# Order of products and of state updates in the scan phase of a two-mixer linear-attention block

## The chip, the cores and the metric

One core of one Trainium2 chip runs the whole layer as one program. The metric is the device time of one execution in microseconds (us); a kernel's time is the median of its runs.

## What is computed

The layer reads 2048 latent tokens and a prefix of 256 context tokens, 1024 channels each. After a modulated norm and one wide projection, two linear-attention mixers run over both, each in both directions: GLA (a decay for each key channel) and Gated DeltaNet (GDN, a decay for each head and the delta rule). The part of the reference that the change touches, cut to its core:

```
def gla_chunked(q, k, v, g, s0):                 # 4 heads, key width 64, value width 128
    bc = cumsum(g within a chunk)
    def step(s, (qi, ki, vi, bi)):
        dec = exp(where(causal, bi[t] - bi[s], -inf))          # for each key channel
        att = einsum('bhtd,bhsd,bhtsd->bhts', qi, ki, dec)
        o = (qi * exp(bi)) @ s + att @ vi
        s_new = s * exp(bl) + (ki * exp(bl - bi)).T @ vi
def gdn_chunked(q, k, v, g, beta, s0):           # 4 heads, widths 128
    ...                                          # u, w, aqk solved ahead of the scan
    def step(s, (qi, ki, ui, wi, ai, gi)):
        v_new = ui - wi @ s
        o = (qi * exp(gi)) @ s + ai @ v_new
        s_new = s * exp(gl) + (ki * exp(gl - gi)).T @ v_new
oa = gla(forward) + rev(gla(backward));  ob = gdn(forward) + rev(gdn(backward))
out = (gate_a * (norm(oa) * silu(ag)) @ w_gla + gate_b * (norm(ob) * silu(bg)) @ w_gdn) @ w_o
return rmsnorm(x + gt * out)
```
Each latent scan starts from the last context state of its own direction. The states after the last latent chunk are not returned.

## The kernel before

The program first projects all tokens (L365, every fp32 product as three products of rounded halves), then convolves, normalises and solves the triangular systems of GDN. The scan phase, `phase_mix`, comes next, and at its end the merge of the mixers (L1519) and the output projection (L1588). All work is written for one core; a scheduler (Tile) sets the order on each engine from the order in which the code issues, and inserts the waits.

Chunks have 128 tokens here: 2 of context and 16 of latents. `phase_mix` makes 17 steps. In step s it prepares GLA's chunk pair (2 + s forward, 17 - s backward), while the scans of the pair that step s - 1 prepared run beside it; the 17th step, the closing one, only scans, beside the first work of the merge. Each piece of work is a Python generator, and `weave` takes them in turn by their weights (12 for `gdn_scan`, 8 for `gla_scan`, 20 for `gla_step`). From the ninth step on both directions of a chunk have been seen, so a finished chunk also runs through `finish` (squares on ScalarE, a product on GpSimd at L1347, transposes at L1352). These steps are the second half below.

GLA's scores inside a chunk (`at`, both directions at once) come level by level: at level m (64, 32, 16, 8, 4, 2, 1) a token pair that a block border of size m separates gets `sum over channels of q * exp(to the border) * k * exp(from the border)`. `gla_group` makes the factors of two levels: sums of gates on TensorE (L1110, fp32r), exponentials on ScalarE (L1192, L1195), the product with q on VectorE (L1201, into `ql`) and with k on GpSimd (L1202, into `E`). `gla_ones` makes level 1, where a factor is the exponential of one token's gate: four transposes (L1213), exponentials (L1215), one VectorE product of 128x256 (L1216). Then `gla_lev` multiplies one level: 64 key channels of one head stand on one half of the rows, so each of its four products uses 64 of the 128 rows of the array (L1226), into one of two slots of the PSUM tile `lv`; a predicated copy on VectorE (L1233), or two copies on ScalarE for level 64 (L1230), takes the pairs of that level into `at`.

`gla_scan` does one chunk in one direction: the update of the 64x128 states in four products that each use half of the columns (L1282), the state read by VectorE, then the output: `at` with v on the whole array (L1306, forward chunk only) and the state product on half of the rows (L1310), added to `prev`, the output of the other direction read back from memory, into `oi`. `gdn_scan` does the same for GDN with whole-array products (L1042, L1053, L1063, L1072 for the state, L1082). `gla_ends`, `gla_kt` and `gla_qe` make the factors at the chunk's ends (L1110, L1128, L1134).

A product of fp32 numbers leaves two records in the trace, a transpose or an fp32r product one. In the profile's rows `64*128` means 64 rows by 128 columns of the array in use; `pz`, `pe` and `pm` are PSUM buffers and `Sa`, `Sb` the states.

Of the kernel before, what the change touches and what calls it, by code (L numbers as in the profile page):

```python
# [11 lines left out]
F32 = mybir.dt.float32  # L12
# [5 lines left out]
ALU = mybir.AluOpType  # L18
# [4 lines left out]
P = 128  # L23
# [7 lines left out]
NCTX = CTX // P  # L31
# [65 lines left out]
class Build:  # L97
# [933 lines left out]
    def gdn_scan(self, r, need_o):  # L1031
# [16 lines left out]
        if need_o:  # L1048
# [5 lines left out]
            oi = self.op.tile(B4, F32, name="oi", bufs=4)  # L1054
# [12 lines left out]
        S2 = self.st.tile(B4, F32, name=f"Sb{d}")  # L1067
        if S is not None:
            nc.gpsimd.tensor_tensor(S2, S, self.bc(self.egl, c, d), op=ALU.mult)
        ps = self.heads(self.pv())  # L1070
        for h in range(4):
            nc.tensor.matmul(ps[:, h], r["kt"][:, h], vn[:, h], start=True, stop=True)  # L1072
        if S is None:
            nc.vector.tensor_copy(S2, ps)
        else:
            nc.vector.tensor_tensor(S2, S2, ps, op=ALU.add)
        self.Sb[d] = S2
        yield
# [90 lines left out]

    def gla_ctx(self, pairs):  # L1170
# [35 lines left out]
    def gla_ones(self, r):  # L1206
        nc, k = self.nc, r["k"]
        E = self.gE.tile([P, 2, P], F32, name="E1", bufs=1)
        ql = self.gq.tile([P, 2, P], F32, name="ql1", bufs=1)
# [6 lines left out]
        nc.vector.tensor_tensor(ql, E, r["q"], op=ALU.mult)  # L1216
        return [(r["at"], [k[:, ct] for ct in range(2)], ql, 1)]

    def gla_lev(self, at, ks, ql, m):
        nc = self.nc  # L1220
        ps = self.slot()
        at = self.byhalf(at)
        for ct in range(2):
            for hp in range(2):
                rows = slice(64 * hp, 64 * hp + 64)
                nc.tensor.matmul(ps[:, hp, ct], ks[ct][rows], ql[rows, ct], start=True, stop=True)  # L1226
        if m == 64:
            for x in range(2):
                rows, cols = slice(64 * x, 64 * x + 64), slice(64 - 64 * x, 128 - 64 * x)
                nc.scalar.copy(at[rows, :, :, cols], ps[rows, :, :, cols])  # L1230
        else:
            i = LEVELS.index(m) - 1
            nc.vector.copy_predicated(at, self.am[:, i].unsqueeze(1).unsqueeze(1).broadcast_to([P, 2, 2, P]), ps)  # L1233

    def gla_step(self, f, b):
# [9 lines left out]
        todo = yield from self.gla_group(f, 0)  # L1245
        self.gla_ends(b)
        yield
        todo += yield from self.gla_group(f, 2)
# [3 lines left out]
        self.gla_lev(*todo.pop(0))  # L1252
        yield
        more = self.gla_group(f, 4)
        next(more)
        yield
        self.gla_lev(*todo.pop(0))
        yield
        try:
            next(more)  # L1260
            next(more)
        except StopIteration as e:
            todo += e.value
        yield
        self.gla_kt(b)
        self.gla_lev(*todo.pop(0))
        yield
        todo += self.gla_ones(f)
        self.gla_qe(f)
        while todo:  # L1270
            yield
            self.gla_lev(*todo.pop(0))
        yield

    def gla_scan(self, r, need_o):
        nc, wk = self.nc, self.wk
        d, c = r["d"], r["c"]
        S = self.Sa[d]
        ps = self.pv()
        for h in range(4):  # L1280
            ct, hp = h // 2, h % 2
            nc.tensor.matmul(ps[64 * hp:64 * hp + 64, ct * P:(ct + 1) * P], r["kt"][:, 64 * h:64 * h + 64],  # L1282
                             r["v"][:, h * P:(h + 1) * P], start=True, stop=True)
        S2 = self.st.tile([P, 2, P], F32, name=f"Sa{d}")
        for ct in range(2):
# [349 lines left out]
```

## Time and profile before

| what | value |
|---|---|
| median of 3 runs | 2199.81 us (2198.74 to 2201.21) |
| profiled execution | 2198.7 us, span 2196.9 us, mean granted clock 0.989 |
| scan phase in the trace | about 1375 to 1805 us |
| L1110 in it, both halves of the gates | 74.3 + 67.2 us busy |
| L1226, both kinds of factors | 68.7 + 11.4 us busy, 15.2 idle ahead |
| L1282, L1306, L1310 | 27.0, 18.1, 15.6 + 14.1 us busy |
| bytes moved | 315.68 MB, mean 144 GB/s |

The engines are named PE (TensorE; PEld is its loading of weights), DVE (VectorE), ACT (ScalarE), POOL (GpSimd) and SP (SyncE, which issues the DMAs). Busy time of PE counts each record from its start to its modelled end, and records overlap: a record of 128 columns counts with about 0.27 us. So the pace is read from the starts. A row `A <- B at L: us, times, us each` of the waits says that A's engine stood idle, and that B's instruction at line L ended that wait.

### The profile page before, as it was taken

What the parts mean: (1) busy time and instruction counts of PE and PEld (TensorE: products, weight loads), DVE (VectorE), ACT (ScalarE), POOL (GpSimd) and SP (SyncE); (2) the same over time, 40 slices, a digit from 0 to 9 for tenths busy, and PEclk for the clock granted to TensorE, in tenths of its full rate; (3) what the DMA queues carried; (4) which work ended last, traced back from release to release, by engine and by line L of the source; (5) the groups of instructions that cost most, each with busy time, mean ns of one, the idle gap of its engine ahead of it and who ended that gap; (6) DMA issues with size and microseconds to landing.
All of it is one profiled execution on the core that took longest, in us unless ns stands there. A gap on an engine that the chain in (4) does not pass through costs nothing. (4 is left out here: it accounts for less than half of the span.)

```text
span 2196.9 us, 40078 instructions
## 1 busy us (share of the span) xinstructions
PE 2122.3 (97%) x15168; PEld 1764.3 (80%) x15168; DVE 1245.2 (57%) x2178; ACT 884.2 (40%) x2188; POOL 858.2 (39%) x765
## 2 busy tenths in 40 slices
PE   5999999999999999999999998999999988999998
PEld 2688888888888888777777776888878877999888
DVE  3813555567776554655555554666777776444333
ACT  3654255455542223443434443444544444111211
POOL 2410122222320115665666662555555554322331
PEclk8999999999999999999999999999999999999999
DMA  8323122222222234443444435888688858433322
GB/s 281 104 89 115 53 60 68 63 63 61 70 75 74 83 89 137 140 141 116 134 150 145 146 134 174 281 303 277 227 267 287 263 176 254 138 120 125 101 80 84
DMA packets 275005, 315.68 MB, mean 144 GB/s; under 512 B 22280, under 2 KB 206716, under 8 KB 274812
## 3 DMA queue, kind: packets, MB, share of 16 engines
q1 hardware_dynamic: 274812, 313.12, 44.4%
q8 instruction: 120, 1.97, 0.4%
q14 instruction: 73, 0.60, 0.1%
HBM read 203.20 MB, written 109.84 MB: 142 GB/s over the span
## 5 line engine op out<-in xcount | busy, mean ns | idle before, releaser
L365 PE MATMUL pz<-hi,wh 128*128 128x512 f32 (+1 forms) x1560 | 621.3, 399 | 1.7 <-DVE hi L133 1.7
L365 PE MATMUL pz<-lo,wh 128*128 128x512 f32 (+1 forms) x1560 | 600.3, 385 | 1.8 <-POOL lo L134 1.8
L365 PE MATMUL pz<-hi,wl 128*128 128x512 f32 (+1 forms) x1520 | 588.0, 387 | 0.0
L365 PEld LDWEIGHTS pz<-lo,wh 128*128 128x128 f32 x1560 | 294.5, 189 | 51.0 <-POOL lo L134 3.6
L365 PEld LDWEIGHTS pz<-hi,wh 128*128 128x128 f32 x1560 | 294.2, 189 | 48.0 <-DVE hi L133 2.5
L365 PEld LDWEIGHTS pz<-hi,wl 128*128 128x128 f32 x1520 | 286.2, 188 | 53.7 <-issue 0.4
L134 POOL TENSOR_TENSOR wl<-w,wh 128x1024 fp32r<-128x1024 f32 x44 | 110.6, 2514 | 436.2 <-ACT wh L131 311.9
L563 DVE SCALAR_TENSOR_TENSOR acc<-zpad,cw,acc 128x1024 f32<-128x1024 f32 x192 | 268.2, 1397 | 6.7
L1519 PE MATMUL pm<-yh,wab 128*128 128x256 f32 x1024 | 187.9, 284 | 4.4 <-DVE mt L1523 4.4
L867 DVE CAST_PREDICATED U<-kit,pl 128x256 f16<-128x256 int32 x216 | 91.3, 432 | 138.7 <-PE pl L990 134.9
L1519 PEld LDWEIGHTS pm<-yh,wab 128*128 128x128 f32 x1024 | 161.3, 193 | 5.1 <-ACT wo L131 4.7
L1588 PE MATMUL pz<-wo,mh 128*128 128x512 f32 (+1 forms) x528 | 161.2, 388 | 0.0
L1519 PE MATMUL pm<-yl,wab 128*128 128x256 f32 x512 | 145.7, 285 | 0.8 <-POOL yl L134 0.8
L983 ACT CAST ppb<-pl 128x256 f16<-128x256 f32 x216 | 73.6, 374 | 166.4 <-PE pl L982 160.0
L1588 PEld LDWEIGHTS pz<-wo,mh 128*128 128x128 f32 x528 | 98.4, 189 | 20.2
L134 DVE TENSOR_TENSOR sql<-sq,sqh 128x512 fp32r<-128x512 f32 (+1 forms) x36 | 28.0, 805 | 141.6 <-ACT sqh L131 141.4
L618 POOL TENSOR_TENSOR acc<-acc,sq 128x512 f32<-128x512 f32 x32 | 50.2, 1576 | 138.4 <-ACT sq L617 78.6
L1588 PE MATMUL pz<-wo,ml 128*128 128x512 f32 (+1 forms) x264 | 101.8, 386 | 0.0
L1519 PEld LDWEIGHTS pm<-yl,wab 128*128 128x128 f32 x512 | 98.7, 193 | 1.7 <-POOL yl L134 1.2
L1202 POOL TENSOR_TENSOR E<-E,ak 128x256 f32<-128x256 f32 x96 | 76.8, 820 | 58.9 <-ACT E L1192 44.7
L134 POOL TENSOR_TENSOR yl<-wr,yh 128x1024 fp32r<-128x1024 f32 x16 | 40.3, 2542 | 134.2 <-ACT yh L131 134.2
L1233 DVE COPY_PREDICATED at<-am,lv 128x512 f32<-128x512 int32 x96 | 70.5, 734 | 31.5 <-PE lv L1226 29.4
(292 smaller groups left out, 4190.5 us busy)
## 6 DMA issues: line engine op xcount, KB each, us to landing
dgate<-ob SPq DMA_DIRECT2D x96, 256.0 KB
gd<-dgd SPq DMA_DIRECT2D x32, 768.0 KB
w<-in_w_in SPq DMA_DIRECT2D x44, 512.0 KB
qk<-dqkv SPq DMA_DIRECT2D x32, 512.0 KB
ga<-dgate SPq DMA_DIRECT2D x64, 256.0 KB
dqkv<-acc SPq DMA_DIRECT2D x192, 64.0 KB
dgd<-tm SPq DMA_DIRECT2D x36, 256.0 KB
dgd<-n SPq DMA_DIRECT2D x36, 256.0 KB
```

The lines of the kernel that those rows point to most:

```text
L134: getattr(nc, lo).tensor_tensor(dst_lo, src, dst_hi.bitcast(F32), op=ALU.subtract)
L365: nc.tensor.matmul(ps[:, 0:n], a[:, kk, :], b[:, kk, :], start=(k == 0), stop=(k == last - 1))
L563: nc.vector.scalar_tensor_tensor(acc, src, wcol, acc, op0=ALU.mult, op1=ALU.add)
L618: nc.gpsimd.tensor_tensor(v, v, r, op=ALU.mult)
L867: self.nc.vector.copy_predicated(out, mv, data)
L983: nc.scalar.copy(ppl, pc.rearrange("p h (j i) -> p h j i", i=m))
L1202: nc.gpsimd.tensor_tensor(E[:, :, li, 1], E[:, :, li, 1], k, op=ALU.mult)
L1233: nc.vector.copy_predicated(at, self.am[:, i].unsqueeze(1).unsqueeze(1).broadcast_to([P, 2, 2, P]), ps)
L1519: nc.tensor.matmul(ps[:, half * 256:half * 256 + 256], wab[wi][:, k, j * P:(j + 1) * P], yy[:, k, :], start=(i == 0), stop=(i == 11))
L1588: nc.tensor.matmul(ps, aa[:, k, i * P:(i + 1) * P], wo[k][wi][:, cs], start=(j == 0), stop=(j == 23))
```

## The change

1. `gla_lev` takes two levels at once: eight half-row products one after the other, then their evictions.
2. `gla_scan` is split. `gla_state` updates both directions' states in one run of eight half-column products (L1303), and is called from inside `gla_step` of the next pair. `gla_out` makes the outputs of both chunks in one run: four whole products (L1321) and eight half-row ones (L1326, directly ahead of the first two levels), into two PSUM tiles, and two VectorE additions into one tile `og`. `prev` of both chunks is one tile too. `gla_step`'s weight goes from 20 to 24.
3. Level 1 is no longer a product of matrices. For neighbours t and t - 1 the score of a head is the sum over its 64 channels of `q * k * exp(gate)`. `gla_ones` makes that elementwise product (two VectorE halves at L1224, and GpSimd with k at L1225), and `gla_near` sums it over the two halves of the rows by a product with a 128x2 matrix of ones and zeros, `bones` (L1232), of which a predicated copy (L1234) takes the right entries.
4. In the closing step GDN's last states are not updated (`end=True`: no L1070, L1073), nor GLA's (`gla_end` calls `gla_out` alone).

The names below carry the numbers that the two programs give to their tiles. TensorE in a first-half step, before: the second half of the levels, from the first product of the next scan (L1042) on.

```order
L1042 MATMUL pz<-Sb_16664,qk 128x128
L1226 MATMUL lv<-ql,E 128x128 x4
L1042 MATMUL pz<-Sb_16664,qk 128x128 x3
L1042 MATMUL pz<-Sb_16672,qk 128x128
L1226 MATMUL lv<-ql,E 128x128 x4
L1042 MATMUL pz<-Sb_16672,qk 128x128 x3
L1110 MATMUL pe<-wt,gh_16819 128x256
L1110 MATMUL pe<-wt,gl_16820 128x256
L1110 MATMUL pe<-wt,gh_16819 128x256
L1226 MATMUL lv<-ql,E 128x128 x4
L1110 MATMUL pe<-wt,gl_16820 128x256
L1282 MATMUL pz<-av,akt 64x128 x7
```
After, the same place:

```order
L1042 MATMUL pz<-Sb_16945,qk 128x128
L1220 MATMUL pe<-kf,g_16785 128x128
L1244 MATMUL lv<-ql,E 128x128 x8
L1220 MATMUL pe<-kf,g_16785 128x128 x3
L1042 MATMUL pz<-Sb_16945,qk 128x128 x3
L1042 MATMUL pz<-Sb_16953,qk 128x128 x4
L1244 MATMUL lv<-ql,E 128x128 x8
L1232 MATMUL pe<-bones,qk_17064 128x2 x2
L1111 MATMUL pe<-wt,gh_17118 128x256
```
The half-row products stand in groups of eight instead of four, and the next step's first gate sums (L1111) now stand behind L1232. Earlier in the same step, after:

```order
L1083 MATMUL pz<-vn,gd 128x128 x8
L1321 MATMUL pz<-av,at 128x128 x4
L1326 MATMUL pz<-Sa_16557,q_16484 128x128 x4
L1326 MATMUL pz<-Sa_16560,q_16490 128x128 x4
L1244 MATMUL lv<-ql,E 128x128 x8
L1111 MATMUL pe<-wt,gh_16813 128x2x128
```
Outputs and the first two levels form one run of 16 half-row products. GpSimd in a second-half step, before (L1202 is the factor with k, L1347 the finishing product, L1134 `gla_qe`):

```order
L1347 TENSOR_TENSOR oi<-oi,fss 128x512
L1202 TENSOR_TENSOR E<-E,ak_19271 128x2x128 x2
L1347 TENSOR_TENSOR oi<-oi,fss 128x512
L1134 TENSOR_TENSOR q_19273<-E_19327,q_19273 128x256
L1347 TENSOR_TENSOR oi<-oi,fss 128x512
L134 TENSOR_TENSOR gl_20085<-g_20056,gh_20084 128x512
```
After:

```order
L1209 TENSOR_TENSOR E<-E,ak_18478 128x2x128 x2
L1384 TENSOR_TENSOR og<-og,fss 128x512
L1225 TENSOR_TENSOR qk_18751<-qk_18751,ak_18478 128x256
L1135 TENSOR_TENSOR q_18480<-E_18534,q_18480 128x256
L1384 TENSOR_TENSOR oi<-oi,fss 128x512 x2
L134 TENSOR_TENSOR gl_19273<-g_19244,gh_19272 128x512
L1384 TENSOR_TENSOR og<-og,fss 128x512
```
The new product L1225 stands behind the first finishing product and ahead of `gla_qe`. ScalarE in that step, after:

```order
L1381 ACTIVATE fy,fss<-og 128x128 x3
L1381 ACTIVATE fy,fss<-oi 128x128
L1382 ACTIVATE fss<-fss,cb 128x4
L1381 ACTIVATE fy,fss<-oi 128x128
L1383 ACTIVATE fss<-fss 128x4
L1222 ACTIVATE E_18750<-pe 128x128 x2
```
Level 1's exponentials (L1222) stand behind the squares of the finishing work.

The diff, cut to its core:

```diff
-    def gdn_scan(self, r, need_o):
+    def gdn_scan(self, r, need_o, end=False):
...
-            oi = self.op.tile(B4, F32, name="oi", bufs=4)
+            oi = self.op.tile(B4, F32, name="oi")
...
+        if not end:
             S2 = self.st.tile(B4, F32, name=f"Sb{d}")
...
     def gla_ones(self, r):
...
-        nc.vector.tensor_tensor(ql, E, r["q"], op=ALU.mult)
-        return [(r["at"], [k[:, ct] for ct in range(2)], ql, 1)]
+        for d in range(2):
+            nc.vector.tensor_tensor(w[:, :, d:P:2], E[:, :, 1 - d:P:2], q[:, :, 1 - d:P:2], op=ALU.mult)
+        nc.gpsimd.tensor_tensor(w, w, k, op=ALU.mult)
+        return w
+
+    def gla_near(self, at, w):
+        nc = self.nc
+        pd = self.pe()
+        for ct in range(2):
+            nc.tensor.matmul(pd[:, 2 * ct:2 * ct + 2], w[:, ct], self.bones, start=True, stop=True)
+        B = [P, 4, P]
+        nc.vector.copy_predicated(at, self.am[:, len(LEVELS) - 2].unsqueeze(1).broadcast_to(B),
+                                  pd[:, 0:4].unsqueeze(2).broadcast_to(B))
+
+    def gla_lev(self, levs):
+        nc, got = self.nc, []
+        for at, ks, ql, m in levs:
+            ps = self.slot()
...
+            got.append((self.byhalf(at), ps, m))
+        for at, ps, m in got:
...
-    def gla_step(self, f, b):
+    def gla_step(self, f, b, prev):
...
+        if prev is not None:
+            S = self.gla_state(prev)
+            yield
+        levs = yield from self.gla_group(f, 0)
         self.gla_ends(b)
         yield
+        more = yield from self.gla_group(f, 2)
         self.gla_kt(f)
         self.gla_qe(b)
         yield
+        if prev is not None:
+            done = self.gla_out(prev, S)
+        self.gla_lev(levs)
+        if prev is not None:
+            done()
+            yield
+            yield from self.gla_put(prev)
+        yield
+        last = yield from self.gla_group(f, 4)
+        yield
+        self.gla_lev(more)
         yield
         self.gla_kt(b)
+        w = self.gla_ones(f)
         self.gla_qe(f)
+        yield
+        self.gla_lev(last)
+        yield
+        self.gla_near(f["at"], w)
+        yield
...
+    def gla_out(self, pair, S):
+        nc = self.nc
+        f = pair[0]
+        po = [self.pv().rearrange("p (d c t) -> p d c t", d=2, c=2) for _ in range(2)]
         for h in range(4):
+            nc.tensor.matmul(po[h % 2][:, 0, h // 2], f["at"][:, h], f["v"][:, h * P:(h + 1) * P],
+                             start=h < 2, stop=False, skip_group_check=True)
+        for d, r in enumerate(pair):
             for h in range(4):
                 ct, rows = h // 2, slice(64 * (h % 2), 64 * (h % 2) + 64)
+                nc.tensor.matmul(po[h % 2][:, d, ct], r["qe"][rows, ct], S[d][rows, ct], start=False,
+                                 stop=d == 1 and h >= 2, skip_group_check=True)
...
-                for (a, b) in prev:
-                    gens.append((self.gdn_scan(b, True), 12))
-                    gens.append((self.gla_scan(a, True), 8))
+                for x in prev:
+                    gens.append((self.gdn_scan(x[1], True, si == len(order)), 12))
+                if si == len(order):
+                    gens.append((self.gla_end(pair), 4))
...
-                gens.append((self.gla_step(*[x[0] for x in cur]), 20))
+                gens.append((self.gla_step(*[x[0] for x in cur], pair if si else None), 24))
```

More of the change, by code (lines that the diff above doesn't have):

```diff
@@ L1066, in gdn_scan @@
         yield
[L1067 to L1078, printed above, removed]
+        if not end:
+            S2 = self.st.tile(B4, F32, name=f"Sb{d}")
+            if S is not None:
+                nc.gpsimd.tensor_tensor(S2, S, self.bc(self.egl, c, d), op=ALU.mult)
+            ps = self.heads(self.pv())
+            for h in range(4):
+                nc.tensor.matmul(ps[:, h], r["kt"][:, h], vn[:, h], start=True, stop=True)
+            if S is None:
+                nc.vector.tensor_copy(S2, ps)
+            else:
+                nc.vector.tensor_tensor(S2, S2, ps, op=ALU.add)
+            self.Sb[d] = S2
+            yield
         if need_o:
@@ L1168, in ctx_loads, with gla_ctx_states @@
         return [[(self.gla0[d, d ^ i], gdn[d, d ^ i]) for d in range(2)] for i in range(2)], rest
+    def gla_ctx_states(self, pairs):
+        for p in pairs:
+            self.gla_state([x[0] for x in p])
+            yield
+            yield
     def gla_ctx(self, pairs):
@@ new lines, in gla_step, with gla_state @@
+        self.gla_lev(last)
+        yield
+        self.gla_near(f["at"], w)
+        yield
+    def gla_state(self, pair):
+        nc = self.nc
+        S = list(self.Sa)
+        ps = self.pv()
+        for d, r in enumerate(pair):
+            for h in range(4):
+                ct, hp = h // 2, h % 2
+                nc.tensor.matmul(ps[64 * hp:64 * hp + 64, (2 * d + ct) * P:(2 * d + ct + 1) * P],
+                                 r["kt"][:, 64 * h:64 * h + 64], r["v"][:, h * P:(h + 1) * P], start=True, stop=True)
+        for d, r in enumerate(pair):
+            S2 = self.Sa[d] = self.st.tile([P, 2, P], F32, name=f"Sa{d}")
+            for ct in range(2):
+                pc = ps[:, (2 * d + ct) * P:(2 * d + ct + 1) * P]
+                if S[d] is None:
+                    nc.vector.tensor_copy(S2[:, ct], pc)
+                else:
+                    nc.vector.scalar_tensor_tensor(S2[:, ct], S[d][:, ct], r["dec"][:, ct:ct + 1], pc,
+                                                   op0=ALU.mult, op1=ALU.add)
+        return S
@@ new lines, in gla_out, with gla_put, gla_end, gla_prev @@
+        return done
+    def gla_put(self, pair):
+        for d, r in enumerate(pair):
+            yield from self.put_o(0, r["c"] - NCTX, self.og[:, d])
+    def gla_end(self, pair):
+        self.gla_out(pair, self.Sa)()
+        yield
+        yield from self.gla_put(pair)
+    def gla_prev(self, pair):
+        ls = [r["c"] - NCTX for r in pair]
+        if ls[0] not in self.seen[0]:
+            pair[0]["prev"] = None
+            return
+        t = pair[0]["prev"] = self.op.tile([P, 2, 4, P], F32, name="prevg", bufs=1)
+        for d, l in enumerate(ls):
+            self.nc.sync.dma_start(self.flat(t[:, d]), self.d_o[0][l])
@@ L1322, in prev_o @@
             return None
-        t = self.op.tile([P, 4, P], F32, name="prev", bufs=4)
+        t = self.op.tile([P, 4, P], F32, name="prev")
         self.nc.sync.dma_start(t.rearrange("p h t -> p (h t)"), self.d_o[i][l])
@@ L1383, in phase_mix @@
         mp = self.pool("mix", 1, ctx=gctx)
+        self.bones = mp.tile([P, 2], F32, name="bones")
+        for x in range(2):
+            nc.vector.memset(self.bones[64 * x:64 * x + 64, x:x + 1], 1.0)
+            nc.vector.memset(self.bones[64 * x:64 * x + 64, 1 - x:2 - x], 0.0)
         self.am = mp.tile([P, len(LEVELS) - 1, P], I32, name="am")
```

103 lines of the change are left out of this document (26 added, 77 removed).

## The prediction

> **What bounds the kernel now.** I read the page's first part, then TensorE's own rows over the scan phase (about 1375 to 1805 us, the only stage that the change touches), then its waits. One window is one step of the scan, from one group of L1213 to the next.
>
> ```profile
> PE 2122.3 (97%) x15168; PEld 1764.3 (80%) x15168; DVE 1245.2 (57%) x2178; ACT 884.2 (40%) x2188; POOL 858.2 (39%) x765
> ```
> ```profile
> core 0: us, PE busy (x) PEld busy (x) DVE busy (x) ACT busy (x) POOL busy (x), PEclk, DMA share, GB/s
> 1350.00:1375.00 25.00, 20.20 (x163) 15.73 (x161) 7.43 (x14) 8.64 (x24) 8.48 (x9) 0.88 0.67 222
> 1495.21:1519.54 24.33, 23.56 (x218) 20.96 (x217) 17.10 (x32) 11.60 (x46) 13.31 (x16) 1.00 0.89 299
> 1543.87:1568.18 24.31, 23.55 (x219) 20.95 (x218) 17.10 (x32) 11.70 (x46) 13.10 (x15) 1.00 0.73 233
> 1676.89:1705.43 28.54, 26.58 (x234) 22.99 (x233) 20.81 (x47) 14.35 (x76) 16.99 (x19) 1.00 0.90 295
> ```
> A step of the first half takes 24.3 us and one of the second half 28.5; TensorE is busy for 23.6 and 26.6 of them, VectorE for 17.1 and 20.8, at full granted clock. So TensorE's queue sets the step, and what it does inside these 23.6 us matters. Its rows in the middle of a first-half step:
>
> ```profile
> 1482.73 1.05 PE L1063 MATMUL pz<-rhs,gd 128*128 128x128 f32 x8
> 1483.62 1.11 PE L1306 MATMUL pz<-av,at 128*128 128x128 f32 x8
> 1484.66 0.71 PE L1310 MATMUL pz<-Sa,q 64*128 64x128 f32 x8
> 1485.30 1.16 PE L1063 MATMUL pz<-rhs,gd 128*128 128x128 f32 x8
> 1486.39 0.71 PE L1310 MATMUL lv<-Sa,q 64*128 64x128 f32 x8
> 1487.03 0.38 PE L1110 MATMUL pe<-wt,gh 128*128 128x256 f32 x1
> ```
> ```profile
> L1226 PE MATMUL lv<-ql,E x768: 272/272/373, 1385.0 to 1798.9; 64*128 64x128 f32 x192
> ```
> Whole-array records (128*128) follow each other at (1483.62 - 1482.73)/8 = 0.11 us. Half-height records (64*128) run in pairs: 0.71 less one record's 0.27 puts the last pair 0.44 after the first, that is three steps of 0.11 and 0.10 over, the 373 against 272 ns of the first pair. Between 1483.62 and 1487.03 lie 3.41 us for 16 whole records (1.78) and 8 pairs (0.90); 0.73 is left, and 0.10 more sits in the first L1110 (0.38 where the others have 0.28). That is 0.83 for four changes of shape: **0.2 us for each change**, in either direction. A whole record starts late after a half-height group and the one after it starts late again.
>
> The Trainium skill, page "TensorEngine Tiling (Array Packing)", section Tiling Modes, says of this that changing the tiling mode, and not just the tile, drains TensorE. A drain alone, the next product starting when the last has ended, would be 0.27 - 0.11 = 0.16 us by the rows above, and the switch term below would be 28 instead of 36 us; the trace agrees on the cause and shows the larger size, so the rows are used.
>
> TensorE's waits in five first-half steps, and then in six second-half steps:
>
> ```profile
> PE lv L1226 <- DVE at L1233: 3.8, 5, 0.8
> ```
> ```profile
> PE lv L1226 <- ACT at L1230: 6.1, 6, 1.1
> PE pe L1352 <- POOL oi L1347: 4.2, 12, 0.5
> PE lv L1226 <- DVE at L1233: 1.4, 6, 0.2
> ```
> So 0.8 us a step, and (6.1 + 4.2 + 1.4)/6 = 1.95 us a step.
>
> **The change, term by term.** The sum is made against the profiled execution, 2198.7 us (span 2196.9); the median of the runs is 1.1 us above it.
>
> 1. *Changes of shape.* I counted them along TensorE's order of both programs: 346 in the scan phase before, 168 after. A steady first-half step goes from 20 to 8, a second-half step from 22 to 12. The price is 178 x 0.2 = 35.6 us. Six of them lie in the opening step and eleven in the closing one, where TensorE waits anyway (20.20 of 25 busy in the window from 1350; the closing rows below): 17 x 0.2 = 3.4 are worth nothing there. Term: **-32.2** (bounds: -26 if a change costs only a record's 0.27 less its 0.11 pace, 0.16; -37 at 0.21 with nothing hidden).
>
> 2. *Level 1.* Four half-height products (8 records, 4 pairs, 0.45 us) go; two products of 2 columns (4 records) come. The nearest rows are the same kind of product in an earlier stage, and records of the scan's doubled product:
>
> ```profile
> L899 PE MATMUL pe<-bones,R x64: 165/251/251, 875.8 to 1307.0; 128*128 128x2 f32 x64
> L1216 DVE TENSOR_TENSOR ql<-E,q 128x256 f32<-128x256 f32 x14 | 10.3, 736 | 1.5 <-ACT E L1215 1.5
> L1215 ACT ACTIVATE E<-pe 128x128 f32<-128x128 f32 x28 | 7.1, 341 | 0.6 <-PE pe L1213 0.6
> L1202 POOL TENSOR_TENSOR E<-E,ak 128x256 f32<-128x256 f32 x87 | 69.8, 821 | 55.5 <-ACT E L1192 42.4 <-ACT E L1195 13.0
> L1347 POOL TENSOR_TENSOR oi<-oi,fss 128x512 f32<-128x512 f32 x21 | 23.8, 1135 | 1.3 <-ACT fss L1346 1.3
> ```
> L899's 0.25 against 0.27 says that a 2-column record is hardly shorter than one of 128 columns, so I price it at the 0.11 pace: 4 x 0.11 = 0.45, **0** in sum (bounds: -0.4 a step if they cost nothing, +0.6 if each took its whole 0.25). VectorE's one product of 736 ns becomes two halves (0.7 in sum); GpSimd gets one more product of 0.82 a step, 13 us in all, beside 13.1 of 24.3 and 17.0 of 28.5 busy: not a bound by its sum, but it now stands in a chain (term 4).
>
> 3. *No state update for the last chunks.* The rows of the closing step:
>
> ```profile
> 1799.72 0.87 PE L1282 MATMUL pz<-av,akt 128*64 128x128 f32 x10
> 1801.17 0.65 PE L1282 MATMUL pz<-av,akt 128*64 128x128 f32 x6
> 1803.08 2.05 PE L1053 MATMUL pz<-Sb,qk 128*128 128x128 f32 x16 [1.26 <-DVE rhs L1045]
> 1818.90 2.05 PE L1072 MATMUL pz<-vn,gd 128*128 128x128 f32 x16 [1.29 <-DVE vn L1065]
> 1820.71 0.36 PE L1519 MATMUL pm<-yh,wab 128*128 128x256 f32 x1
> 1835.73 0.36 PE L1519 MATMUL pm<-yh,wab 128*128 128x256 f32 x1 [1.49 <-DVE mt L1523]
> 1841.72 0.36 PE L1519 MATMUL pm<-yh,wab 128*128 128x256 f32 x1 [2.88 <-DVE mt L1523]
> ```
> L1072 (1.8 us, 1818.90 to 1820.71) and L1282 (0.87 + 0.65 less the overlap of 0.27 each, 1.0) go: 2.8 us. Around them stand 6.9 us of TensorE's waits for VectorE, which loses only some small operations there, so most of it becomes waiting: **-1.0** (bounds 0 and -2.8).
>
> 4. *Order and waits.* The eviction of one group of two levels now has other work behind it before the next group needs the buffers, so the 0.8 at L1233 should shrink; but the last product of a step, L1232, waits for GpSimd, and every later product is queued behind it. Its chain starts at the transposes (L1220): 0.27 for them, two exponentials, two VectorE halves, the GpSimd product. A row for ScalarE's pace:
>
> ```profile
> 1470.87 0.80 ACT L1195 ACTIVATE E<-pe 128x128 f32<-128x128 f32 x4 [0.41 <-PE pe L1110]
> ```
> Four in 0.80, so (0.80 - 0.29)/3 = 0.17 apart: two end after 0.5. Chain: 0.27 + 0.5 + 0.74 + 0.82 + four hand-overs at about 0.1 = 2.7 us. TensorE has 7 products of L1042 (14 records, 1.6) and 8 half-height ones (0.9 + 0.4 for their two changes) between, 2.9 us. First half: no wait to speak of, I allow 0.4: -0.4 a step, 8 steps, **-3.2**. Second half: ScalarE has five squares of the finishing work ahead of the exponentials and GpSimd a product of 1.1 (L1347's row) ahead of its new one, the eviction order puts VectorE between, and the transposes behind L1232 wait for GpSimd as before. I lay the 1.95 us of now at 2.3: +0.35 x 7 = **+2.5** (bounds: -1.95 and +1.5 a step).
>
> DMAs: the same number of issues, the same bytes. At the second half's 0.90 share of 28.54 us the engines need 25.7 us a step; the new step (28.5 - 10 x 0.2 + 0.35 = 26.9) still holds that. State updates of GLA move into the step of the next chunk pair, all of it TensorE and VectorE work of the same size. The double buffers of `oi` and `prev` go from four tiles for four uses a step to two for two: nothing.
>
> Sum: -32.2 + 0 - 1.0 - 3.2 + 2.5 = -33.9. 2198.7 - 33.9 = 2164.8 profiled, 2166 against the median.
>
> **Rivals.**
>
> *A. Half of it is taken back by the wait for GpSimd's product.* For it: five hand-overs in one chain against 2.9 us of cover, and VectorE's products stretch where GpSimd works beside them:
>
> ```profile
> 1693.41 0.75 DVE L1201 TENSOR_TENSOR ql<-E,q 128x256 f32<-128x256 f32 x2
> 1539.52 2.26 DVE L1201 TENSOR_TENSOR ql<-E,q 128x256 f32<-128x256 f32 x2
> ```
> The same two products take 0.75 or 2.26 us. If the stretch of 1.5 falls on L1224 and the products before it in most steps, 15 x 1.2 = 18 us come back: 2184. Against it: the added GpSimd work comes after VectorE's in the chain, not beside it. The Trainium skill, page "GPSIMD Engine Reference", section 1, Specifications, says that GpSimd's SBUF interfaces are shared with VectorE, with contention for instructions that have two SBUF inputs; these two rows agree in direction.
>
> *B. Slower.* One mechanism: L1232 holds TensorE's queue in the second half and the first alike until GpSimd has served the finishing products (1.1 each) and the chain. It decides from 34/15 = 2.3 us a step beyond what I allow; at 3 us the time is 2166 + 45 - 2 = 2209. It needs both GpSimd's queue and VectorE's stretch at their worst in every step; the first half has no finishing products. Unlikely.
>
> *C. More than forecast.* The waits vanish in both halves (another -0.4 x 8 and -2.3 x 7): 2166 - 19 = 2147. For it: ScalarE and VectorE have a quarter of the step free.
>
> *D. No change.* The groups might be split again by the scheduler, or the transfers be the real limit. The order shows the groups whole, and TensorE's rows leave no idle time for a hidden limit in the first half. The share of 0.9 in the second half could cost 0.4 a step, 3 us, inside the range.
>
> **Chances.** Forecast (2155 to 2177) 0.62; A (2177 to 2193) 0.17; C (below 2155) 0.10; D 0.04; B 0.07. The range of 2152 to 2189 leaves out most of C's far end, B and D. A difference of 0.2%, 4.4 us, is about what these runs can tell from none. Faster 0.89, same 0.04, slower 0.07; the forecast alone spans 2155 to 2177.
>
> **What the new profile would show.** Right: first-half steps of about 21.6 us, second-half steps of about 26.9; only one pair in sixteen records of L1244 at 373 ns; VectorE's busy time per step about as now, so its share above 0.75; the wait of L1232 for L1225 below 0.5 us in the first half. Wrong: that wait above 1.5 us a step (A, B), long waits of L1244 for L1253, or DMA landings as the releasers of TensorE in the second half.

## The result, and the profile after

The changed kernel takes 2182.05 us (median of 4 runs, 2181.01 to 2187.47) against 2199.93; the ratio is 0.9923, 95% interval 0.9907 to 0.9939. That is 17.9 us less where 34 were forecast: the direction held, the size was half. In a later comparison on another chip the same kernel gave 0.9924 [0.9913, 0.9936]. Two of the variants below (the first and the seventeenth) ran their profiled execution at a clock of 0.56, so only their times are used.

The page's first part of the kernel after, and one window for each of three steps (two of the first half, one of the second; a step now runs from L1220 to L1220):

```profile
PE 2091.0 (96%) x15072; PEld 1749.6 (80%) x15072; DVE 1243.7 (57%) x2183; ACT 881.0 (40%) x2180; POOL 866.6 (40%) x779
```
```profile
core 0: us, PE busy (x) PEld busy (x) DVE busy (x) ACT busy (x) POOL busy (x), PEclk, DMA share, GB/s
1491.17:1513.88 22.71, 21.65 (x213) 20.04 (x213) 15.66 (x32) 11.31 (x46) 13.77 (x16) 1.00 0.91 284
1513.88:1539.38 25.50, 22.18 (x213) 20.15 (x213) 15.64 (x32) 11.09 (x46) 13.77 (x16) 1.00 0.75 262
1665.96:1693.69 27.73, 24.97 (x230) 22.27 (x228) 23.03 (x47) 14.26 (x76) 17.81 (x22) 1.00 0.97 301
```
TensorE is busy for 21.7 us of a first-half step instead of 23.6, and for 25.0 of a second-half step instead of 26.6. But it is idle for 1.1 us of the first (0.8 before), 3.3 of the second, and 2.8 of the third (2.0 before). Its waits over the scan phase, first before, then after:

```profile
PE lv L1226 <- ACT at L1230: 7.6, 7, 1.6
PE lv L1226 <- DVE at L1233: 7.6, 17, 0.8
PE pe L1352 <- POOL oi L1347: 4.9, 14, 0.5
```
```profile
PE pe L1389 <- POOL oi L1384: 6.8, 11, 0.7
PE lv L1244 <- DVE at L1253: 6.4, 10, 0.9
PE pe L1232 <- POOL qk L1225: 6.3, 8, 1.0
PE pz L1073 <- DVE vn L1065: 4.5, 6, 1.3
...
PE pz L1321 <- DVE oi L1084: 3.5, 8, 0.6
```
The waits of the half-row products fell from 15.2 to 6.4 us, more than the 0.4 us a first-half step that was forecast. Four that were small or absent took their place: for GpSimd's product of level 1 (L1232), for GDN's `vn` (L1073), for a PSUM buffer of the outputs (L1321), and more at the finishing transposes (L1389).

Where the time went, from the starts of all of TensorE's records over the 15 steps between the first and the last transposes of the gates. Each distance from one start to the next is split into the pace of its kind (0.111 us whole, 0.056 half-row, 0.0545 half-column, 0.12 for a gate sum) and the rest, which is counted as a wait where it is over 0.2 us:

| us | before | after | difference | in the first eight steps | in the next seven |
|---|---|---|---|---|---|
| products at their pace | 308.9 | 312.3 | +3.4 | +2.4 | +1.0 |
| changes of shape (312, then 150) and of type | 61.6 | 29.6 | -32.0 | -17.3 | -14.7 |
| waits | 26.9 | 42.4 | +15.5 | +9.5 | +6.0 |
| the 15 steps | 397.4 | 384.4 | -13.0 | -5.4 | -7.7 |

(The pieces sum to the length within 0.3 us.) The border between a change and a wait is a choice: with idle time of over 0.2 us ahead of a record as the mark of a wait, the changes fall by 28 us and the waits grow by 12. Of the +3.4, 3.1 us are 20 whole records and 16 half-column ones, mostly one set of state products, that stand ahead of the first of these 15 steps before the change and inside it after. With 1.6 us ahead of the first step and 2.4 behind the last, the -13.0 makes the 17.1 us between the two spans. The first eight steps went from 199.1 to 193.7 us, the next seven from 198.3 to 190.6; here they are before, then after:

```profile
1393.41:1592.50 199.09, 192.76 (x1786) 168.72 (x1785) 135.83 (x252) 95.19 (x360) 108.28 (x125) 1.00 0.80 274
1592.50:1790.83 198.33, 183.95 (x1611) 159.39 (x1610) 145.12 (x319) 98.38 (x506) 113.19 (x127) 1.00 0.80 259
```
```profile
1391.78:1585.52 193.74, 180.62 (x1781) 164.19 (x1779) 130.78 (x265) 92.77 (x354) 113.14 (x131) 1.00 0.82 285
1585.52:1776.15 190.63, 172.82 (x1598) 155.83 (x1599) 152.99 (x320) 95.13 (x485) 114.13 (x132) 0.99 0.84 268
```
TensorE is idle for 13.1 us of the first eight steps instead of 6.3, and for 17.8 of the next seven instead of 14.4. So two thirds of the 10.2 us of new idle time lie in the first eight steps.

### The profile page after: what moved, and what is told of

It is laid out like the page before. It is cut to its first block, busy times and chain, and to the rows that moved or that the text cites. A ratio compares the mean times of both kernels' runs of the same rounds, so it can differ in the third digit from the quotient of the medians.

```text
span 2179.8 us, 39740 instructions
## 1 busy us (share of the span) xinstructions
PE 2091.0 (96%) x15072; PEld 1749.6 (80%) x15072; DVE 1243.7 (57%) x2183; ACT 881.0 (40%) x2180; POOL 866.6 (40%) x779
## 5 line engine op out<-in xcount | busy, mean ns | idle before, releaser
L1636 POOL TENSOR_TENSOR xo<-xo,mt 128x512 f32<-128x512 f32 x30 | 44.6, 1486 | 104.0 <-DVE mt L1635 92.9
```

The source lines that it names most:

```text
L1636: (nc.vector if end else nc.gpsimd).tensor_tensor(xs, xs, sq, op=ALU.add)
```

## The experiments

Ratios are to the kernel before, from runs on the same chip.

**e1, e2: the wait for level 1's product taken away.** e1 issues `gla_ones` ahead of the last group, e2 issues the sum in the next step:

```diff
+        w = self.gla_ones(f)
         last = yield from self.gla_group(f, 4)
```
```diff
             S = self.gla_state(prev)
+            self.gla_near(prev[0]["at"], prev[0]["w"])
```


> Level 1's elementwise product is prepared one group earlier in the step (its transposes ahead of the last two levels' gate sums), so TensorE has more work between the transposes (L1220) and the sum (L1232). Theory A (the chain through ScalarE, VectorE and GpSimd is what L1232 waits for, 6.3 us in the changed kernel's trace, and the finishing transposes L1389 wait longer because GpSimd serves L1225 first): the wait of L1232 falls below 1 us in the scan phase and the time to 2173 to 2177 us. Rival B (the steps are held by another chain, so a wait taken away here comes back elsewhere): L1232's wait goes, other waits grow by as much, 2180 to 2184 us.

> The sum over channels (L1232) and its predicated copy move into the next step, behind GLA's state products; the elementwise product stays where it is. Theory A: L1232 no longer waits for GpSimd (below 1 us in all), 2173 to 2177 us, as with the early product. Rival B: 2180 to 2184 us. If the early product gains and this one does not, it is not the wait but where the work on ScalarE, VectorE and GpSimd lies.

Measured: 2191.23 us, 0.9947 [0.9934, 0.9960], and 2190.01 us, 0.9941 [0.9927, 0.9955]: no better than the changed kernel, and slower than both theories gave. TensorE's waits of e2 from 1610 to 1790 us:

```profile
PE pe L1390 <- POOL og L1385: 10.1, 11, 1.3
PE pe L1390 <- POOL oi L1385: 9.8, 10, 1.3
```
L1232's wait is gone, and the finishing transposes (here L1390) wait 19.9 us where L1389 waited 6.6 in the second half. TensorE only came sooner to a product that was no earlier. Theory A fell for the second half; rival B's mechanism held, though not its time.

**e3: level 1 by half-row products again**, the rest as changed (`gla_ones` as before; `gla_near(f["at"], w)` becomes `gla_lev(w)`).

> Level 1 is again made by four half-row products as before the change, all else as in the changed kernel; its products stand apart from those of the other levels, which adds two changes of shape a step. Theory A: the wait for GpSimd at L1232 (6.3 us) and part of the longer waits of the finishing transposes go, 16 x 2 x 0.19 = 6 us of shape changes come, 2178 to 2185 us, no clear difference. Rival C (the elementwise form is the change's real gain): 2190 us or more. Rival D (it is the real loss, beyond the wait): 2174 us or less.

Measured: 2193.69 us, 0.9967 [0.9956, 0.9978]. Beside parts 1 and 2 the elementwise form is worth some 9 us, wait and all, as rival C says; by the estimate above 6 of them are the two added changes of shape a step.

**e4: state update and outputs in a generator of their own.**

```diff
+    def gla_both(self, pair):
+        S = self.gla_state(pair)
+        yield
+        self.gla_out(pair, S)()
...
-                gens.append((self.gla_step(*[x[0] for x in cur], pair if si else None), 24))
+                gens.append((self.gla_step(*[x[0] for x in cur]), 20))
```


> State update and outputs of GLA are a generator of their own again, woven beside the scans as before the change, still both chunks in one run each; gla_step's weight is 20 again. Theory E (the outputs and state products that moved were the cover for GDN's waits for VectorE: L1073 4.5 us and L1321 3.5 us in the changed kernel's trace): these waits fall below 2 us together, and two more changes of shape a step come, 15 x 2 x 0.19 = 6 us: 2178 to 2183 us. Rival B: other waits take their place and the shape changes come on top, 2186 us or more.

Measured: 2191.07 us, 0.9956 [0.9942, 0.9971]; its order has 165 changes of shape in all, not the 30 more that I counted on. Its waits in five first-half steps (1444 to 1590 us), and those of the changed kernel in the same stretch:

```profile
PE pe L1111 <- ACT E L1120: 4.0, 3, 1.9
PE lv L1244 <- DVE at L1253: 3.1, 6, 0.6
PE pe L1232 <- POOL qk L1225: 0.8, 1, 0.8
```
```profile
PE pz L1073 <- DVE vn L1065: 4.1, 5, 1.3
PE pz L1321 <- DVE oi L1084: 2.7, 6, 0.6
```
The first half of theory E is shown: with the state products back between L1063 and L1073 both waits are gone. But 7.9 us of waits at three other places stand against the 6.8 of these two and 2.3 at L1111 and L1244, and the five steps take 115.4 us against 117.2. In the second half L1244 then waits 12.8 us for VectorE, more than before, and the granted clock is 0.91 from 1612 to 1785 us, where the changed kernel's is 0.97 to 1.00: at half for 48 us of the 15 steps, where the changed kernel has 3. So e4 is as slow as rival B says, but in part by its clock, and its time tells little on the rest of theory E.

**e5: the changed kernel again.**

> The changed kernel itself once more, so that the variants can be held against it on one chip: ratio to the kernel before 0.990 to 0.994, its steps as in the first trace, the step of 25.5 us at the same place.

Measured: 2184.36 us, 0.9924 [0.9913, 0.9936], the long step at its place (25.57 us).

**e6: part 1 alone**, on the kernel before (`gla_lev(todo[:2])` and so on, with the new `gla_lev`).

> The kernel before with part 1 of the change alone: two levels of half-row products at once, all else (outputs, state updates, level 1, the closing step) as before. It has 248 changes of shape in TensorE's order against 341 before and 160 after. Theory G (a change of shape costs 0.19 us, and the moves of parts 2 and 3 gave their share back in waits): 93 x 0.19 = 18 us less than before, as much as the whole change brought, ratio 0.990 to 0.994. Rival H (the gain is in parts 2 and 3, and two evictions behind one group make the next group wait): ratio 0.995 or more.

Measured: 2201.56 us, 1.0008 [0.9998, 1.0017]: 93 changes of shape fewer, and nothing gained. It gains 10 us in the first eight steps (188.9 us against 199.1, where the whole change gains 5.4) and loses 12 in the next seven (210.4 against 198.3). A first-half step, a second-half step, and 6 us from the end of the latter on (columns as above); then TensorE's and ScalarE's rows around its start:

```profile
1535.87:1558.58 22.71, 22.54 (x216) 20.39 (x216) 16.95 (x31) 11.47 (x47) 13.00 (x15) 1.00 0.77 248
1668.65:1699.28 30.63, 27.66 (x233) 25.04 (x233) 22.28 (x46) 14.70 (x76) 16.77 (x19) 0.89 0.84 271
...
1699.00:1705.00 6.00, 5.72 (x33) 4.94 (x33) 4.57 (x8) 2.79 (x16) 4.39 (x5) 0.50 0.39 130
```
```profile
1695.92 0.39 PE L1042 MATMUL pz<-Sb,qk 128*128 128x128 f32 x2
1699.28 0.48 PE L1213 MATMUL pe<-kf,g 128*128 128x128 f32 x1 [2.97 <-ACT E L1195]
```
```profile
1695.26 0.31 ACT L1346 ACTIVATE fy<-oi 128x128 f32<-128x128 f32 x1 [1.57 <-DVE oi L1083]
...
1697.68 0.73 ACT L1232 COPY at<-lv 64x256 f32<-64x256 f32 x2
1698.43 1.48 ACT L1195 ACTIVATE E<-pe 128x128 f32<-128x128 f32 x8
```
ScalarE stands at a square of the finishing norm (L1346) until VectorE has the output; level 64's copies and the last exponentials are in line behind it, and TensorE waits 2.97 us for a PSUM buffer. Then its clock is granted at half for the next 6 us and more, so the wait is paid a second time; the seven steps have 38 us at half clock in all, and those of the kernel before none.

The first eight steps tell what parts 2 and 3 add there: they take out 46 more changes of shape (112 to 66, some 9 us), and TensorE's idle time goes from 3.8 us in e6 to 13.1 in the changed kernel.

**e7: early merge weights held back.**

```diff
-                self.raws = [self.out_raw(j) for j in range(2)]
+                self.raws = [self.out_raw(j, self.Sa[0][:, 0, 0:1]) for j in range(2)]
...
+        if after is not None:
+            for x in (0, 4):
+                nc.gpsimd.tensor_copy(raw[:, x, 0:1], after)
```


> The changed kernel, but the first four loads of merge weights (256 KB each), which the scheduler issues in the middle of the first half, are held back until the state of the last step but one exists, by a one-column copy into their tiles. All other engines' orders in the first half are the same. Theory F (the 25.5 us step is long because these loads stand ahead of the gates' load): that step falls to about 22.9 us, 2.6 us in all, ratio lower by 0.001. Rival: the step stays at 25 us or more, and the gates' load is late for another reason.

Measured: 2182.14 us, 0.9913 [0.9900, 0.9926] (beside e5's 0.9924). The long step of e5, and the same one of e7:

```profile
1516.32:1541.89 25.57, 22.18 (x212) 20.15 (x212) 15.66 (x32) 11.09 (x46) 13.77 (x16) 1.00 0.74 267
```
```profile
1514.33:1537.68 23.35, 21.65 (x212) 20.04 (x213) 15.65 (x32) 11.10 (x46) 13.77 (x16) 1.00 0.74 242
```
2.2 us less in this step: the loads ahead of the gates' were its cause. On the whole time the intervals overlap.

**e8: the finishing transposes later in TensorE's queue.**

```diff
+            gens += [(g, 8) for g, _ in fin]
             self.weave(gens)
-            self.weave(self.fin)
+            fin, self.fin = self.fin, []
+            for g, _ in fin:
+                next(g)
```


> The changed kernel, but the transposes of the finishing work (L1389) are issued a quarter into the next step, between GDN's products, instead of right behind L1232. Theory I (in the second half the finishing chain through ScalarE and GpSimd starts later than before the change, since both chunks' outputs come together at the end of a step, and TensorE's queue is held at L1389): the waits at L1389 (6.6 us in the second half) fall below 2 us, and 2174 to 2178 us against 2182, ratio about 0.989. Rival B (another wait takes their place): no faster than the changed kernel.

Measured: 2182.33 us, 0.9917 [0.9904, 0.9930], no faster. L1389's waits for GpSimd fell from 8.7 us (e5) to 0.3 in the scan phase, and L1321 and L1063 took 3 and 5 us more: rival B again.

**e9, e15, e16: without ScalarE's part of the finishing norm.** The squares, the logarithm and the exponential are left out; e9 and e15 on e6, e16 on e7.

```diff
-        for h in range(4):
-            nc.scalar.activation(sq[:, h], src[:, h], AF.Square, accum_out=ss[:, h:h + 1])
-        nc.scalar.activation(ss, ss, AF.Ln, bias=self.eps, scale=1.0 / 128)
-        nc.scalar.activation(ss, ss, AF.Exp, scale=-0.5)
+        ss = self.beta[:, 2, 0:4]
```


> Part 1 alone again (groups of two levels on the kernel before), and the squares, logarithm and exponential of the finishing norm are left out (its scale is set to one), so ScalarE's queue has no instruction that waits for a finished output. TensorE's order is the same as with part 1 alone. There TensorE stood 3.0 us in each second-half step at the transposes L1213, and its clock then ran at half for some 6.8 us. Theory J (ScalarE's squares, in line ahead of the last exponentials, hold TensorE): wait and half clock go, second-half steps fall from 30.7 to 26 to 27 us (28.5 less 8 changes of shape at 0.19), ratio 0.983 to 0.990. Rival K (the grouped evictions or the PSUM buffers hold it): the steps stay above 29 us, ratio 0.997 or more.

> Part 1 alone, without the squares, logarithm and exponential of the finishing norm (its scale is a tile that is there already, so nothing is written for it). Theory J (ScalarE's squares wait for VectorE's finished outputs in line ahead of level 64's copies and the last exponentials, and TensorE waits for these): second-half steps fall from 30.7 to 26 to 27.5 us, ratio 0.983 to 0.990. Rival K (they stay above 29 us, held by the grouped evictions on VectorE): ratio 0.997 or more.

> The changed kernel, early merge weights held back, without the squares, logarithm and exponential of the finishing norm (its scale is a tile that is there already). Theory J for the changed kernel (ScalarE's queue stands 39 us of the second half at squares that wait for og, with level 64's copies and exponentials behind them): second-half steps fall from 27.5 to 25 or 26 us, ratio 0.983 to 0.987. Rival (GpSimd's and VectorE's finishing work alone holds the steps): 27 us or more, ratio above 0.989.

e9 set the scale with a memset on VectorE, which had to wait for GpSimd's finishing product (17.0 us of VectorE's waits), so it put the same chain into another engine's queue: 1.0008 [0.9991, 1.0024], TensorE waiting 17.8 us for VectorE instead. It tells nothing on ScalarE alone, but shows that the same chain in VectorE's queue holds TensorE as well. e15: 2177.88 us, 0.9893 [0.9880, 0.9907], the seven second-half steps 186.0 us instead of 210.4. e16: 2169.62 us, 0.9861 [0.9844, 0.9878], seven steps of 177.6 us against 191.8 in e7. ScalarE's longest wait from 1610 us on in e7, and in e16; then the first and the last of four second-half steps of e16 that follow each other:

```profile
ACT fy L1381 <- DVE og L1336: 40.3, 6, 6.9
```
```profile
ACT at L1250 <- PE lv L1244: 38.7, 6, 6.6
```
```profile
1606.85:1633.49 26.64, 25.97 (x246) 23.56 (x247) 22.21 (x48) 9.36 (x39) 20.31 (x23) 1.00 0.89 289
...
1684.00:1708.89 24.89, 23.38 (x212) 21.13 (x211) 20.27 (x45) 7.71 (x31) 16.43 (x20) 1.00 0.90 293
```
Without this work the changed kernel is 31 us (0.0139 of 2201) faster than the kernel before with it. That is near the forecast in size, but not the change's own gain: the kernel before was not run without this work. The DMA share is 0.89 to 0.90 in these two steps (0.95 and 0.96 in the two between): the transfers allow 25.5 us a step (1606.85 to 1708.89 in four).

Theory J is shown as far as that ScalarE's finishing work lengthens the seven steps, by 24 us in part 1 alone and by 14 in the changed kernel. For the changed kernel its mechanism is not: ScalarE stands still for as long in e16, now at level 64's copies (L1250) for their products, and in a typical step these copies start 0.48 us after the outputs' last product there and 1.12 us in e7. What goes are TensorE's waits for GpSimd in these steps, 6.7 us at the finishing transposes (L1389) and 3.8 at L1232 in e7, none in e16; and e7 has 6.8 us at half clock there, e16 none.

**e10: part 3 alone**, on the kernel before.

> The kernel before with part 3 alone (level 1 by the elementwise product and the sum over channels), 339 changes of shape against 341. In TensorE's order the sum now stands 7 products behind the transposes of the gates, about 1.2 us of work. Theory A (chain of transposes, exponentials, VectorE, GpSimd of 2.7 us by the prediction, 3.8 to 4.2 us in the changed kernel's trace): a wait of 1.5 to 3 us in each of 16 steps, 2215 to 2240 us, ratio 1.007 to 1.02. Rival (the product is ready in time, or the wait replaces those that TensorE has now): ratio 0.997 to 1.003.

Measured: 2237.48 us, 1.0175 [1.0156, 1.0193], as theory A says. The waits of its scan phase:

```profile
PE pe L1225 <- POOL qk L1218: 20.9, 14, 3.3
PE lv L1237 <- POOL oi L1360: 10.0, 6, 1.7
```
20.9 us at the sum (here L1225) and, behind GpSimd's finishing product, 10.0 at `lv`; half clock follows in most second-half steps.

**e11: parts put together.** First eight steps as e6, the later ones as e7.

```diff
+                    if si < 8:
+                        gens.append((self.gla_scan(x[0], True), 8))
...
+                gens.append((self.gla_step1(*x), 20) if si < 8 else (self.gla_step(*x, pair), 24))
```


> A version put together from the runs so far: the first eight steps with part 1 alone (outputs and state updates between GDN's products as before the change, level 1 by half-row products), the later steps as in the changed kernel, and the early loads of merge weights held back. First eight steps 189 us as with part 1 alone against 193 to 197 in the changed kernel, the rest as there: 2173 to 2178 us, ratio 0.987 to 0.990, faster than both. Rival B (what the first half gains is waited for at the seam): ratio 0.991 to 0.993.

Measured: 2182.44 us, 0.9923 [0.9908, 0.9937], like the changed kernel: the first eight steps took 191.1 us, 2.2 more than in e6, and the first began 2 us later.

**e12: part 4 alone.**

> The kernel before with part 4 alone: no state updates in the closing step. One look, at the stretch from the last L1213 to the end (406.1 us before, 403.7 in the changed kernel). The prediction's term is -1.0 us. If the stretch falls by 2 us or more, the closing step gave more than forecast; if it stays at 406, VectorE's chain holds it.

The stretch from the last transposes of the gates on, before and in e12:

```profile
1790.83:2196.90 406.07, 387.83 (x2526) 351.83 (x2524) 189.58 (x301) 89.31 (x220) 127.06 (x111) 0.99 0.41 130
```
```profile
1790.16:2194.70 404.54, 383.98 (x2494) 348.86 (x2492) 194.29 (x295) 89.48 (x220) 127.40 (x111) 0.99 0.41 131
```
1.5 us less, in one run.

**e13, e14: VectorE freed from a wait for stores.** e13 is e7 with the finishing product written over its gate tile; e14 adds e2's edit.

```diff
-        gt = wk.tile([P, 4, P], F32, name="fg", bufs=2)
+        gt = wk.tile([P, 4, P], F32, name="fg", bufs=4)
...
-        y = wk.tile([P, 4, P], F32, name="fy")
+        y = gt
```


> The changed kernel with the early merge weights held back, and the finishing product (L1391) writes over its gate tile (four of them instead of two) instead of into one of two buffers that it shares with the squares, so VectorE no longer waits there for a store to land. Theory L (VectorE, held at L1391 by these stores, is what makes TensorE's waits come back elsewhere in the second half): VectorE's wait for the store of y falls from 9.4 us to below 1, second-half steps from 27.6 to 26.5 us, ratio 0.987 to 0.989. Rival B: the wait goes and the steps stay at 27.5 us, ratio 0.990 to 0.993.

> As the run before, and the sum over channels (L1232) stands in the next step as in the second run. If theory L holds, the wait for GpSimd now counts and another 0.5 us a step goes: ratio 0.984 to 0.987. Rival M (taking L1232 away only lets TensorE arrive earlier at the finishing transposes, which wait for GpSimd's product of the same chain): no better than the run before, waits at L1389 of 10 us or more in the second half.

Measured: 2183.53 us, 0.9928 [0.9915, 0.9940], and 2187.32 us, 0.9936 [0.9923, 0.9950]. VectorE's 9.4 us of waits for stores are gone and the time is the same: theory L fell. In e14 L1390 waits 16.2 us in the second half, as rival M says.

**e17, e18: all work kept, the finishing work woven into the next step.** e17 on e7; e18 on e6 with part 4 and the weights held back.

```diff
+            gens += [(g, 6) for g, _ in fin]
             self.weave(gens)
-            self.weave(self.fin)
-            self.fin = []
+            fin, self.fin = self.fin, []
```


> The changed kernel, early merge weights held back, all work kept, but the whole finishing work of a step is issued woven into the next step, so its squares stand behind level 1's exponentials instead of ahead of level 64's copies in ScalarE's queue. It has 210 changes of shape against 160, since the transposes now fall between half-row groups (50 x 0.19 = 9.5 us). Theory J: second-half steps of 26 to 27 us even so, ratio 0.985 to 0.990. Rival (the place does not matter): ratio 0.993 or more.

> Version for use: the kernel before with parts 1 and 4, the finishing work woven into the next step, and the early merge weights held back; outputs, state updates and level 1 as before the change; 244 changes of shape. If the place of the squares is what cost part 1 its gain: first eight steps about 187 us, second-half steps 26 to 27.5 us, ratio 0.984 to 0.989, faster than the changed kernel. If not, second-half steps of 29 us or more and ratio above 0.993.

Measured: 2183.15 us, 0.9918 [0.9903, 0.9932], between theory and rival, and 2204.82 us, 1.0017 [1.0008, 1.0026], as the second outcome says. In e18 no square stands ahead of level 64's copies in ScalarE's order any more, and its second-half steps still take 30.6 us; the waits are spread now:

```profile
PE lv L1227 <- DVE at L1236: 8.2, 5, 2.4
PE pz L1310 <- DVE vn L1065: 6.5, 6, 1.5
```
So the place of the squares in one queue is not enough of an answer. What e15 and e16 show is what leaving the work out is worth; whether its length on ScalarE, its hand-over to GpSimd, or another order that the scheduler made of the rest gives the gain stays open. No version that keeps all the work beat the changed kernel beyond the intervals.

## Why half of the forecast gain came

*Step 1, changes of shape: right.* 162 fewer in the 15 steps gave 32.0 us, 0.2 each, as was used (0.17 if idle time marks a wait). The trace shows it in place:

```profile
1539.38 0.33 PE L1220 MATMUL pe<-kf,g 128*128 128x128 f32 x1
1539.63 1.16 PE L1244 MATMUL lv<-ql,E 64*128 64x128 f32 x16
1540.73 0.55 PE L1220 MATMUL pe<-kf,g 128*128 128x128 f32 x3
...
1543.87 0.61 PE L1232 MATMUL pe<-bones,qk 128*128 128x2 f32 x4
```
Eight pairs take 1.10 (1539.63 to 1540.73), that is 0.90 and one change.

*Step 2, level 1: the products right, the chain's price too low.* The products at their pace moved by 3.4 us in all, 3.1 of them by the set of state products that changed sides, so level 1 itself cost next to nothing. But the chain from L1220 to L1232 takes 4.49 us here and 3.85 in the second-half step below, where I put 2.7. I had not counted that half-row products stand between the first transpose and the other three, nor that an eviction (L1253, at 1541.91) stands between VectorE's two halves (L1224, at 1541.70 and 1542.53); in the second half VectorE's halves take 1.31 beside GpSimd's finishing product instead of the 0.74 that I used:

```profile
1665.96 0.66 PE L1220 MATMUL pe<-kf,g 128*128 128x128 f32 x4
1667.56 1.04 POOL L1384 TENSOR_TENSOR og<-og,fss 128x512 f32<-128x512 f32 x1 [0.70 <-POOL E L1209]
1667.64 1.31 DVE L1224 TENSOR_TENSOR qk<-E,q 128x128 f32<-128x128 f32 x2
1669.81 0.61 PE L1232 MATMUL pe<-bones,qk 128*128 128x2 f32 x4 [0.76 <-POOL qk L1225]
```
In the steady first-half steps the cover grew as well, and nothing waits; in the second half L1232 waits 0.76 us in the step shown, and 6.3 us in the whole scan phase.

*Step 3, the closing step: about right.* -1.0 was forecast, e12 shows -1.5 in one run.

*Step 4, order and waits: this is the step that failed.* It came to -0.7 us in sum, -3.2 for the first half and +2.5 for the second; the waits grew by 15.5, +9.5 in the first eight steps and +6.0 in the next seven (+6.8 and +3.4 in idle time alone; 2.2 of the first are the load in the next paragraph). So the first-half term was the one most wrong. I followed the one chain that the change adds and the one wait that it removes, and did not ask what the moved outputs had covered. Before, they stood between L1063 and L1072; in the changed kernel TensorE waits there for VectorE's `vn` (4.1 us at L1073 from 1444 to 1590 us) and at the outputs' new place for a PSUM buffer (2.7 at L1321), where the kernel before waits at neither. e4 shows the cause of these two: with other products in between, both are gone. For the second half I took the finishing work as a neighbour of level 1's chain only. Without ScalarE's part of it, 14 us of those seven steps go (e16 against e7), 10.5 of them TensorE's waits for GpSimd at L1389 and L1232. How much of this the change itself brought is open: the kernel before waits 4.2 us at the same transposes (L1352), and was not run without the work.

*The DMAs at nothing:* wrong by 2.2 us in one step (e7), where the gates' load stood behind four others. The issues are as many as before, but in the changed kernel these four stand together, from 1506.4 to 1508.0 us, ahead of the gates' load at 1517.0; before, they were issued from 1496.8 to 1502.2, 13 us ahead of it, and TensorE did not wait for it.

*Rival A* came nearest in time (2184), half of the gain taken back; its mechanism is there (6.3 us at L1232), but that is 6.3 of some 16 us lost, and with that wait gone (e2, e14) nothing was gained; that its time came near is luck. Of the signs I named, VectorE's share above 0.75 did not come (15.66 of 22.71 is 0.69), and the steady first-half steps are 22.7 to 23.3 us (one is 25.5) instead of 21.6. The second-half steps came near: 27.2 on average, where 26.9 was forecast.

## What to carry to other kernels

Price what a moved instruction covered at its old place, not only what it waits for at the new one: the 32 us of the order itself came as counted, and waits took back 10 to 15, most of them in steps for which fewer waits had been forecast. A wait taken away from an in-order queue is a gain only if the next instruction's data are already there; before removing one, look at what the instructions behind it wait for. A queue that stands still for long need not be the one that costs: ScalarE stood 40.3 us in e7 and 38.7 in e16, and the steps of e16 were 2 us shorter. Parts of one change need not add up: alone, part 1 gave nothing and part 3 cost 37 us, and the whole change gained 18.

## What the hardware showed that was not expected

In e6 a wait of TensorE of some 3 us is paid twice. A few half-microsecond windows around the wait that ends at 1699.28:

```profile
1698.50:1699.00 0.50, 0.00 (x0) 0.00 (x0) 0.50 (x1) 0.50 (x4) 0.00 (x0) 0.79 0.96 389
1699.00:1699.50 0.50, 0.22 (x1) 0.18 (x1) 0.25 (x2) 0.50 (x5) 0.00 (x0) 0.50 0.92 356
...
1705.50:1706.00 0.50, 0.50 (x12) 0.50 (x12) 0.00 (x0) 0.50 (x1) 0.00 (x0) 0.88 0.55 131
```
The last record ahead ends at 1696.3 (1695.92 and 0.39, above). A mean of 0.79 over the half microsecond from 1698.5 puts the fall to 0.50 at 1698.8, 2.5 us later and ahead of the next product; the 0.88 puts the return at 1705.6. That is 6.8 us at half, by an estimate (half of that time) some 3.4 us more than the wait. The Trainium skill, page "TensorE: Matmul & The Clock Gate", Part 1, has a free-running window of about 3.4 us after which an idle array runs at half and a busy one at full. 6.8 us is two such windows, and in that this trace agrees; but the fall came after 2.5 us without a product, not after a whole idle window. The fall also came without a long gap: in the first trace of the changed kernel TensorE was busy for 0.66, 0.57 and 0.53 in three microseconds running, from 1640.5 on, with waits of 0.77 and 0.58, and the next 3 us ran at 0.53.

```profile
1640.50:1641.50 1.00, 0.66 (x12) 0.46 (x10) 1.00 (x4) 0.75 (x5) 0.57 (x2) 1.00 0.87 252
1641.50:1642.50 1.00, 0.57 (x5) 0.58 (x6) 1.00 (x5) 0.81 (x7) 1.00 (x2) 1.00 1.04 386
1642.50:1643.50 1.00, 0.53 (x5) 0.28 (x4) 1.00 (x3) 0.00 (x0) 1.00 (x2) 1.00 0.70 241
1643.50:1646.50 3.00, 2.90 (x16) 2.24 (x17) 2.35 (x5) 2.48 (x13) 1.86 (x3) 0.53 0.79 244
```
So several short waits close together can do what one long wait does, though the same kernel's second trace has no such place there.

The clock record of the other traces fits both places. In each of the 18 traces used here, the edges of the half-clock stretches lie on a grid of 3.41 us. Cut into windows of 3.41 us on that grid, the time from 1385 to 1800 us of these traces has 2097 windows at full clock. Half clock followed on all 30 windows in which TensorE's records cover less than 45% (0.92 us of the one that ends at 1698.8), on 21 of the 148 between 45 and 70% (2.06 us of the one that ends at 1643.7), and on none of the other 1919. What decides between 45 and 70% stays open.
